# Griffin/PEER step on one core: the sample rows' experts divided over two blocks, four row places, one place for the slot tile

## The chip, the cores and the metric

The kernel runs on one NeuronCore of a Trainium2 chip. The metric is the device time of one execution in microseconds (us). Engines are named as in the profile: PE (matrix multiply, with PEld for its weight loads), DVE (vector), ACT (scalar/activation), POOL (here it issues the gathers by index), SP (it issues most DMAs). Each engine works through its own queue strictly in order, and engines wait for each other through semaphores.

## What is computed

One layer is applied to 1024 prompt rows and to 64 sample rows (8 sequences of 8) with the same weights:

```python
xn = rmsnorm(x)
xr, gr, q, k, v, ga, gb = split(xn @ w_in)
A = (rglru(conv(xr)) * gelu(gr)) @ w_branch_lru        # recurrent branch
B = window_attention(q, k, v) @ w_branch_attn          # sliding window, sinks
h = x + (sigmoid(ga) * A + sigmoid(gb) * B) @ w_out
# PEER on xt = rmsnorm(h): 8 heads x 16 experts out of 128*128 for each row
s = einsum('nhpd,hpkd->nhpk', (xt @ w_query), sub_keys)
idx, g = top16 of the sums of the two halves' top16, softmax
act = gelu(einsum('cd,ced->ce', xt, expert_u[idx])) * g
y = h + einsum('ce,ced->cd', act, expert_v[idx])
```

So each row needs 128 rows of `expert_u` and 128 rows of `expert_v`, chosen by its own scores.

## The kernel before

**Blocks.** The 1088 rows are cut into three blocks (`BLOCKS`), here called block 0 (256 prompt rows and the 64 sample rows), block 1 and block 2 (384 prompt rows each). `trunk(b)` works through one block: attention, the attention branch (its results `mg`, L322), the recurrent part `lru`, the recurrent branch (`th`, L337 and L338), `gh`/`gl` (L345, L346), `w_out` (its sums `hr`, L356), the second norm, and `retrieve` (the query projection and the top-16 search of `s`, L766 to L773). All projections go through `mm3`: three matmuls for each product of operands split in two parts, with weights streamed in pieces of 512 KB (`wraw`, `wlo`). After the three blocks, `dense` runs the prompt rows of blocks 0 and 1 against all 16384 experts, while the rows of block 2 gather theirs.

**Work behind a block.** What block b left for PEER is done during block b+1's trunk as a generator, `behind(b)`. `bg(k)` at each place of the trunk draws k steps from it, k from the table `PG1` while block 1 runs and `PG2` while block 2 runs (places 0 to 7: `mg` chunks, `lru` rounds, second branch, `w_out`, norm, `retrieve`, attention's projections, attention's scores). A scheduler then orders each engine's queue. The steps are:

- `choose(b)`: the candidates of block b's rows are reduced to 16 experts for each head; a step is either a search (max and index) or a pair of an `eq` (L822) and its minimum `ev` (L824). The sample rows come first, and their indices and weights go to `est`.
- for the sample rows alone `early_u` and `early_v`: 64 gathers of 128 rows each from `expert_u`, each multiplied and summed on DVE into one column of `eh` (L963), then gelu on `eh` (L965), then 64 gathers from `expert_v`, accumulated on DVE (L981), two final sums, and the store to `y`. The 64 sample rows stand twice in the 128 partitions, each half with 64 of the 128 experts.
- `build_g(b)`: the expert weights of the block's prompt rows are laid out as a dense table `g_d` for `dense`. It goes by chunks of 32 rows (8 chunks for block 0, 12 for block 1) and in each by products of 4 rows: DVE makes `oi` (L939), `oj` (L940) and `wi` (L941), PE multiplies (L922, four matmuls), ACT copies the result into `sg` (L923), and SP stores `sg` after 8 products (L925). The slot tile `sT` of a chunk is loaded by SP (L929).

**Shared places.** `sg`, the sample rows' gather places `et`, and attention's `at` are one buffer (tag `at`, one place). So `at_free` holds the early steps back until attention is over, and `sg` can't be written before the last reader of `et` is done. In `et`, one quarter holds the rows or the sum, and three quarters hold gathered rows:

```python
xt = et[:, 0:D]
row = et[:, D * (1 + s % 3):D * (2 + s % 3)]
sT = sp.tile([P, 3, CH], F32, tag="sT", name="sT", bufs=2)
```

Of the kernel before, what the change touches and what calls it, by code (L numbers as in the profile page):

```python
# [19 lines left out]
P = 128  # L20
# [41 lines left out]
PG1 = (6, 5, 4, 5, 2, 2, 0, 0)  # L62
PG2 = (5, 5, 4, 3, 2, 2, 2, 1)
# [11 lines left out]
class Kern:  # L75
# [325 lines left out]
    def attention(self, bi, xh, xl, ah, al, raw, bg):  # L401
# [46 lines left out]
        def scores(t, j, qT):  # L448
# [6 lines left out]
            for par in range(2):  # L455

                pss = self.mm().rearrange("p (g s) -> p g s", s=256)
                pr = slice(par * HD, par * HD + HD)
                for g2 in range(2):
                    nc.tensor.matmul(pss[:, g2, 0:S], qT[pr, 2 * j + g2, :], kT[pr, j, c0 + b0:c0 + 2 * P], start=True, stop=True)  # L460
                for g2 in range(2):
                    g = 2 * g2 + par
                    nc.vector.scalar_tensor_tensor(sb[:, g, 0:S], self.distP[:, b0:], -SLOPES[4 * j + g],
                                                   pss[:, g2, 0:S], op0=ALU.mult, op1=ALU.add)
# [312 lines left out]
    def choose(self, bi):  # L777
# [6 lines left out]
        for t, (c0, r) in sorted(enumerate(tiles), key=lambda x: x[1][1]):  # L784
# [31 lines left out]
            bf = xp.tile([P, PH, TOPK], F32, tag="bf", name="bf", bufs=1)  # L816
# [48 lines left out]
    def slots_T(self, ft, r, n0):  # L865

        nc = self.nc
        pt = self.tr((P, 3, P))
        for x in range(3):
            nc.tensor.transpose(pt[:, x, 0:r], ft[0:r, x], self.ident[0:r, 0:r])  # L870
        sl = self.xp.tile([P, 3, P], F32, tag="sl", name="sl", bufs=1)
        nc.scalar.copy(sl[:, :, 0:r], pt[:, :, 0:r])
        nc.sync.dma_start(self.sT_d[:, :, n0:n0 + r], sl[:, :, 0:r])
# [39 lines left out]
    def build_g(self, bi):  # L913
# [13 lines left out]
        for ch in range(COL0[bi] // CH, (COL0[bi] + nP) // CH):  # L927
            sT = sp.tile([P, 3, CH], F32, tag="sT", name="sT", bufs=2)
# [3 lines left out]
            for t4 in range(CH // 4):  # L932
# [5 lines left out]
                oi = sp.tile([P, P, 4], BF16, tag="oi", name="oi", bufs=2)  # L938
# [13 lines left out]
    def early_u(self):  # L952
# [3 lines left out]
        xt = et[:, 0:D]  # L956
        for a in range(2):
            nc.sync.dma_start(et[a * NS:(a + 1) * NS, 0:D], self.xn2n_d[NA:, :])
        for s in range(NSLOT // 2):
            row = et[:, D * (1 + s % 3):D * (2 + s % 3)]  # L960
# [8 lines left out]
    def early_v(self):  # L969
# [3 lines left out]
        acc = et[:, 0:D]  # L973
        row = lambda s: et[:, D * (1 + s % 3):D * (2 + s % 3)]
# [16 lines left out]
    def behind(self, b):  # L991

        early, left = False if b else None, True
        ch = self.choose(b)
        while left or early is not False:
            if early is None and self.es is not None and self.at_free:
                early = itertools.chain(self.early_u(), self.early_v())
            if left:
                left = next(ch, None) is not None
            for _ in range(2):  # L1000
                if early and next(early, None) is None:
                    early = False
# [206 lines left out]
```

## Time and profile before

| | |
|---|---|
| median of 3 runs (each) | 3769.24 us (3769.24, 3769.95, 3755.25) |
| the profiled execution | 3754.26 us, span of its trace 3752.5 us |
| busy share of the span | PE 89%, DVE 77%, POOL 41%, ACT 34% |
| DMA | 1012 MB moved, mean 270 GB/s |
| trunk of the three blocks | from 0 to about 1816 us |
| `dense` | from about 1816 us to the end |

PE's share is an average over stages with different limits. PE counts as busy while matmuls are in its pipeline. The stages of blocks 1 and 2 are read below by windows whose edges are the starts on DVE of the block's first `mg` (L322) and first `gl` (L346), of the end of a block's search (1284 and 1816). "The middle" of a block is the window from its first `mg` to its first `gl` (attention branch, `lru`, second branch), "the tail" what follows it (`w_out`, norm, `retrieve`).

### The profile page before, as it was taken

To read this page: it belongs to the slowest core of one execution; us is meant where nothing else is said; L and a number is where in the kernel's file an instruction comes from. 1 tells how busy PE (TensorE), PEld (TensorE's weight loads), DVE (VectorE), ACT (ScalarE), POOL (GpSimd) and SP (SyncE) were. 2 spreads that over 40 slices of the span, in tenths; PEclk is the share of its full clock that TensorE was granted. 3 is DMA by queue.
4 is the path that set the end of the run, shared out by engine and by line. 5 is a ranking of instruction groups with operands and counts; after the bars stand their busy time and mean duration, and the time that the engine had idled before them with its cause. 6 is when DMAs were issued, how large, how long until landed. Compare 5 with 4: busy or idle time off the path is not lost.

```text
span 3752.5 us, 58800 instructions
## 1 busy us (share of the span) xinstructions
PE 3336.7 (89%) x21891; PEld 3211.5 (86%) x21891; DVE 2882.6 (77%) x6803; ACT 1268.9 (34%) x2331; POOL 1520.3 (41%) x1240
## 2 busy tenths in 40 slices
PE   6899999883058989999889999999999999999996
PEld 6798988883058869998779999999999999999996
DVE  5567797984577988867899787777777776777777
ACT  4555454641033455743222222222222222222221
POOL 0011100223400000000367677677767776777774
PEclk8899999987579999999889999999999999999998
DMA  7388856998747627788488989989989888999988
GB/s 230 99 268 282 284 169 194 326 310 309 234 147 266 199 86 245 247 288 280 160 276 300 310 314 317 314 306 320 320 306 312 308 307 305 318 326 313 306 307 284
DMA packets 551327, 1012.37 MB, mean 270 GB/s; under 512 B 39452, under 2 KB 357852, under 8 KB 547936
## 3 DMA queue, kind: packets, MB, share of 16 engines
q1 hardware_dynamic: 409920, 494.75, 40.9%
q0 software_dynamic: 141120, 513.86, 38.5%
q8 instruction: 172, 2.82, 0.3%
q14 instruction: 115, 0.94, 0.1%
HBM read 904.14 MB, written 105.99 MB: 269 GB/s over the span
## 4 chain that ended last, share of the span: by engine, by line
PE 28%; DMA 18%; DVE 13%; issue 8%; POOL 7%; ACT 2%; SPq 0%; POOLq 0%; DVEq 0%; ACTq 0%
DMA row<-in_expert_v,iA 6%; DMA row<-in_expert_u,iA 4%; PE tr L922 3%; DMA et<-in_expert_v,est 3%; PE ou L183 3%; PE ou L184 3%; PE ou L185 3%; PE mm L185 3%; PE mm L183 3%; PE mm L184 3%; PE sc L183 3%; PE sc L184 3%; PE sc L185 3%; POOL row L888 2%; DVE row L890 2%
## 5 line engine op out<-in xcount | busy, mean ns | idle before, releaser
L183 PE MATMUL ou<-ah,vh 128*128 128x384 f32 (+1 forms) x2048 | 634.0, 314 | 42.5 <-ACT ah L163 20.2
L183 PE MATMUL sc<-dx,uh 128*128 128x256 f32 (+1 forms) x2048 | 637.7, 311 | 19.7 <-DVE al L164 10.3
L185 PE MATMUL sc<-dx,ul 128*128 128x256 f32 (+1 forms) x2048 | 635.9, 311 | 1.0 <-POOL ul L164 1.0
L184 PE MATMUL sc<-dx,uh 128*128 128x256 f32 (+1 forms) x2048 | 636.5, 311 | 0.0
L184 PE MATMUL ou<-al,vh 128*128 128x384 f32 (+1 forms) x2048 | 630.5, 310 | 1.9 <-DVE al L164 1.9
L185 PE MATMUL ou<-ah,vl 128*128 128x384 f32 (+1 forms) x2048 | 629.4, 310 | 0.5 <-POOL vl L164 0.5
L164 POOL TENSOR_TENSOR ul<-un,uh 128x1024 fp32r<-128x1024 f32 x128 | 308.2, 2408 | 790.3 <-ACT uh L163 787.4
L902 DVE SCALAR_TENSOR_TENSOR acc<-row,hv,acc 128x1024 f32<-128x1024 f32 x384 | 493.1, 1284 | 127.5 <-DMA row<-in_expert_v,iA 124.3
L890 DVE SCALAR_TENSOR_TENSOR row<-row,xt 128x1024 f32<-128x1024 f32 x384 | 465.0, 1216 | 138.7 <-DMA row<-in_expert_u,iA 136.5
L900 POOL DMA_INDIRECT row<-in_expert_v,iA x384 | 361.6, 942 | 278.6 <-DVE acc L902 202.9
L888 POOL DMA_INDIRECT row<-in_expert_u,iA x384 | 365.8, 953 | 265.5 <-DVE row L890 186.4
L183 PEld LDWEIGHTS ou<-ah,vh 128*128 128x128 f32 x2048 | 385.6, 190 | 59.8 <-DVE dac L1077 27.1
L183 PEld LDWEIGHTS sc<-dx,uh 128*128 128x128 f32 x2048 | 392.5, 192 | 21.4 <-DVE al L164 11.7
L185 PEld LDWEIGHTS sc<-dx,ul 128*128 128x128 f32 x2048 | 391.9, 191 | 1.5 <-POOL ul L164 1.5
L184 PEld LDWEIGHTS sc<-dx,uh 128*128 128x128 f32 x2048 | 392.3, 192 | 0.0
L184 PEld LDWEIGHTS ou<-al,vh 128*128 128x128 f32 x2048 | 388.1, 190 | 3.6 <-DVE al L164 2.7
L185 PEld LDWEIGHTS ou<-ah,vl 128*128 128x128 f32 x2048 | 387.6, 190 | 0.7 <-POOL vl L164 0.7
L922 PE MATMUL tr<-oij 128*128 128x128 f32 x1280 | 169.3, 288 | 202.4 <-ACT sg L923 200.7
L1077 DVE TENSOR_TENSOR dac<-dac,ou 128x384 f32<-128x384 f32 (+1 forms) x672 | 313.8, 481 | 38.2 <-PE ou L185 37.2
L922 PEld LDWEIGHTS tr<-oij 128*128 128x128 f32 x1280 | 164.6, 204 | 206.9 <-ACT sg L923 202.2
L164 POOL TENSOR_TENSOR vl<-vn,vh 128x1024 fp32r<-128x1024 f32 x128 | 309.2, 2420 | 14.6 <-ACT vh L163 12.6
L163 ACT CAST uh<-un 128x1024 fp32r<-128x1024 f32 x128 | 134.4, 1050 | 459.7 <-PE sc L184 360.9
(295 smaller groups left out, 7357.0 us busy)
## 6 DMA issues: line engine op xcount, KB each, us to landing
wlo<-lo_d SPq DMA_DIRECT2D x168, 512.0 KB, 4.9
wraw<-in_w_in SPq DMA_DIRECT2D x132, 512.0 KB, 5.9
un<-in_expert_uT SPq DMA_DIRECT2D x128, 512.0 KB, 5.9
vn<-in_expert_v SPq DMA_DIRECT2D x128, 512.0 KB, 5.8
lo_d<-wlo POOLq DMA_DIRECT2D x84, 512.0 KB, 6.0
g_d<-sg SPq DMA_DIRECT2D x20, 2048.0 KB, 6.9
wraw<-in_peer_w_query SPq DMA_DIRECT2D x48, 512.0 KB, 6.2
gt<-g_d SPq DMA_DIRECT2D x32, 768.0 KB, 10.3
```

What stands on the lines that cost most here:

```text
L163: nc.scalar.copy(hi, src)
L164: return (lo_eng or nc.vector).tensor_tensor(lo, src, f32(hi), op=ALU.subtract)
L183: nc.tensor.matmul(ps, lh, rh, start=first and j == 0, stop=False)
L184: nc.tensor.matmul(ps, lh, rl, start=False, stop=False)
L185: nc.tensor.matmul(ps, ll, rh, start=False, stop=last and j == n - 1)
L888: nc.gpsimd.indirect_dma_start(out=row, out_offset=None, in_=i["expert_u"], in_offset=bass.IndirectOffsetOnAxis(ap=ia[:, s:s + 1], axis=0))
L890: nc.vector.scalar_tensor_tensor(row, row, 1.0, xt, op0=ALU.mult, op1=ALU.mult, accum_out=hv[:, s:s + 1])
L900: nc.gpsimd.indirect_dma_start(out=row, out_offset=None, in_=i["expert_v"], in_offset=bass.IndirectOffsetOnAxis(ap=ia[:, s:s + 1], axis=0))
L902: nc.vector.scalar_tensor_tensor(acc, row, hv[:, s:s + 1], acc, op0=ALU.mult, op1=ALU.add)
L922: nc.tensor.matmul(pt[:, x, :], oj[:, x], wi[:, x], start=True, stop=True)
L1077: nc.vector.tensor_tensor(ac[k // 4][:, k % 4, a:b], ac[k // 4][:, k % 4, a:b], ps[:, 0:b - a], op=ALU.add)
```

## The change

`early_u` stays behind block 0, and so runs in block 1's trunk; `early_v` now runs behind block 1, in block 2's trunk. One early step is drawn with each step in place of two. `et` now has four places for gathered rows, and the rows `xt` and the sum `acc` have a tile of their own (tag `ex`). The room for it is found by giving `sT` and `oi` one place in place of two, and by letting `bf` share with `fi` and `sl` share with `cd`. The two tables change. In attention's `scores`, the four matmuls go in the order of the heads and so alternate between the two halves of the partitions and between two PSUM banks, and the DVE operations follow all four. Line numbers after L460 are lower by 2 in the changed kernel (L923 is L921 there).

```diff
-PG1 = (6, 5, 4, 5, 2, 2, 0, 0)
-PG2 = (5, 5, 4, 3, 2, 2, 2, 1)
+PG1 = (5, 5, 4, 5, 2, 2, 0, 0)
+PG2 = (6, 6, 5, 1, 2, 4, 2, 2)
...
-            for par in range(2):
-                pss = self.mm().rearrange("p (g s) -> p g s", s=256)
-                pr = slice(par * HD, par * HD + HD)
-                for g2 in range(2):
-                    nc.tensor.matmul(pss[:, g2, 0:S], qT[pr, 2 * j + g2, :], kT[pr, j, c0 + b0:c0 + 2 * P], start=True, stop=True)
-                for g2 in range(2):
-                    g = 2 * g2 + par
-                    nc.vector.scalar_tensor_tensor(sb[:, g, 0:S], self.distP[:, b0:], -SLOPES[4 * j + g],
-                                                   pss[:, g2, 0:S], op0=ALU.mult, op1=ALU.add)
+            pss = [self.mm().rearrange("p (g s) -> p g s", s=256) for _ in range(2)]
+            for g in range(4):
+                pr = slice(g % 2 * HD, g % 2 * HD + HD)
+                nc.tensor.matmul(pss[g % 2][:, g // 2, 0:S], qT[pr, 2 * j + g // 2, :], kT[pr, j, c0 + b0:c0 + 2 * P], start=True, stop=True)
+            for g in range(4):
+                nc.vector.scalar_tensor_tensor(sb[:, g, 0:S], self.distP[:, b0:], -SLOPES[4 * j + g],
+                                               pss[g % 2][:, g // 2, 0:S], op0=ALU.mult, op1=ALU.add)
...
-            bf = xp.tile([P, PH, TOPK], F32, tag="bf", name="bf", bufs=1)
+            bf = xp.tile([P, PH, TOPK], F32, tag="fi", name="bf", bufs=1)
...
-        sl = self.xp.tile([P, 3, P], F32, tag="sl", name="sl", bufs=1)
+        sl = self.xp.tile([P, 3, P], F32, tag="cd", name="sl", bufs=1)
...
-            sT = sp.tile([P, 3, CH], F32, tag="sT", name="sT", bufs=2)
+            sT = sp.tile([P, 3, CH], F32, tag="sT", name="sT", bufs=1)
...
-                oi = sp.tile([P, P, 4], BF16, tag="oi", name="oi", bufs=2)
+                oi = sp.tile([P, P, 4], BF16, tag="oi", name="oi", bufs=1)
...
-        xt = et[:, 0:D]
+        xt = self.sp.tile([P, D], F32, tag="ex", name="xt", bufs=1)
...
-            row = et[:, D * (1 + s % 3):D * (2 + s % 3)]
+            row = et[:, D * (s % 4):D * (s % 4 + 1)]
...
-        acc = et[:, 0:D]
-        row = lambda s: et[:, D * (1 + s % 3):D * (2 + s % 3)]
+        acc = self.sp.tile([P, D], F32, tag="ex", name="eacc", bufs=1)
+        row = lambda s: et[:, D * (s % 4):D * (s % 4 + 1)]
...
-        early, left = False if b else None, True
+        early, left = None, True
...
-                early = itertools.chain(self.early_u(), self.early_v())
+                early = self.early_v() if b else self.early_u()
...
-            for _ in range(2):
-                if early and next(early, None) is None:
-                    early = False
+            if early and next(early, None) is None:
+                early = False
```

On ACT in block 1, at the step from `gh` to `sg`, the queue before was this (`whi` are casts of weight pieces, here all eight of `w_out`):

```order
L345 ACTIVATE gh<-mg 128x384 x6
L208 CAST whi<-wraw 128x1024 x8
L965 ACT_TABLE_LOAD
L965 ACTIVATE eh<-eh 128x64
L923 COPY sg<-tr 128x128x4 x11
L931 CAST s_9206<-sT 128x32
L923 COPY sg<-tr 128x128x4 x8
```

and after the change it is this:

```order
L345 ACTIVATE gh<-mg 128x384 x8
L208 CAST whi<-wraw 128x1024 x2
L963 ACT_TABLE_LOAD
L963 ACTIVATE eh<-eh 128x64
L921 COPY sg<-tr 128x128x4 x6
L929 CAST s_8753<-sT 128x32
L921 COPY sg<-tr 128x128x4 x2
L208 CAST whi<-wraw 128x1024
```

The gelu of `eh` and the first `sg` copies moved from behind all of `w_out`'s weight casts to a place between them, and on DVE the 64 rows of `expert_v` no longer stand between `eh` and the last reader of `et`.

On DVE in block 1, the end of the early rows stood like this before:

```order
L963 SCALAR_TENSOR_TENSOR et,eh<-et 128x1024 x7
L966 TENSOR_TENSOR eh<-eh,est 128x64
L979 TENSOR_SCALAR et<-et,eh 128x1024
L981 SCALAR_TENSOR_TENSOR et<-et,eh 128x1024 x63
L986 TENSOR_TENSOR et<-et 64x1024
L987 TENSOR_TENSOR et<-et 64x1024
L940 TENSOR_TENSOR oij<-iof,sT 128x512
```

and after the change the end of `expert_v`'s rows stands in block 2, ahead of the first `gl`:

```order
L979 SCALAR_TENSOR_TENSOR eacc<-et,eh,eacc 128x1024 x2
L337 SCALAR_TENSOR_TENSOR th<-th,mm 128x384
L979 SCALAR_TENSOR_TENSOR eacc<-et,eh,eacc 128x1024
L338 TENSOR_TENSOR mg<-mg,th 128x384
L337 SCALAR_TENSOR_TENSOR th<-th,mm 128x384
L338 TENSOR_TENSOR mg<-mg,th 128x384
L984 TENSOR_TENSOR eacc<-eacc,et 64x1024
L346 SCALAR_TENSOR_TENSOR gl<-mg,gh 128x384 x3
L985 TENSOR_TENSOR eacc<-eacc,et 64x1024
```

The whole run of 63 rows left block 1's `w_out`, and its rows now stand one to three at a time between the trunk's operations of block 2's middle.

On DVE in block 2 after the change, the step from one chunk of `build_g` to the next behind `w_out` reads like this (`s_14962` and `s_15188` are the casts of the two chunks' `sT`):

```order
L937 TENSOR_TENSOR oi<-iota_208,s_14962 128x512
L939 TENSOR_TENSOR oij<-oi,sT 128x512
L938 TENSOR_TENSOR oij<-iof,sT 128x512 x6
L937 TENSOR_TENSOR oi<-iota_208,s_15188 128x512
L939 TENSOR_TENSOR oij<-oi,sT 128x512
```

and on PE behind `w_out` in block 2 the queue is this:

```order
L183 MATMUL mm<-whi,gh 128x256
L184 MATMUL mm<-wlo,gh 128x256
L185 MATMUL mm<-whi,gl 128x256
L920 MATMUL tr<-oij 128x128 x148
L267 MATMUL tr<-ident,xn 128x128 x8
L920 MATMUL tr<-oij 128x128 x8
```

Before, no more than three products (12 of these matmuls) stood together in block 2; now 37 products (148 matmuls) stand together between `w_out` and the norm's transposes, and the first `oj` of a chunk follows directly on the last `wi` of the chunk before, with one place for `sT`.

Counted in the order of DVE's queue:

| window | early rows (of them final sums) before, after | `oj` | `oi` | `wi` | `eq`/`ev` pairs | searches |
|---|---|---|---|---|---|---|
| middle of block 1 | 46, 60 | 9, 8 | 11, 7 | 9, 6 | 24, 24 | 24, 24 |
| tail of block 1 | 84 (2), 4 | 55, 56 | 53, 57 | 55, 58 | 0, 0 | 1, 1 |
| attention of block 2 | 0, 0 | 0, 0 | 0, 0 | 0, 0 | 8, 15 | 12, 15 |
| middle of block 2 | 0, 65 (1) | 73, 7 | 69, 8 | 67, 7 | 16, 9 | 11, 8 |
| tail of block 2 | 0, 1 (1) | 23, 89 | 27, 88 | 29, 89 | 0, 0 | 0, 0 |

## Rows read from the trace of the kernel before

**Rows 1.** The page: span, and granted TensorE clock in 40 slices (tenths).
```profile
span 3752.5 us, 58800 instructions
...
PEclk8899999987579999999889999999999999999998
```

**Rows 2.** Windows by stage: busy time (and instructions) of each engine, clock, DMA share, GB/s.
```profile
607.00:846.50 239.50, 214.89 (x1131) 204.02 (x1129) 210.26 (x592) 112.84 (x164) 52.38 (x49) 0.94 0.95 312
846.50:1284.00 437.50, 232.30 (x1680) 228.56 (x1680) 300.49 (x857) 106.94 (x186) 78.48 (x79) 0.77 0.70 237
1284.00:1386.00 102.00, 87.00 (x421) 61.41 (x422) 87.75 (x299) 59.14 (x178) 0.00 (x0) 0.93 0.20 60
1386.00:1652.00 266.00, 261.08 (x1656) 254.84 (x1654) 216.74 (x491) 146.15 (x235) 0.00 (x0) 1.00 0.78 255
1652.00:1816.00 164.00, 147.85 (x1018) 145.45 (x1018) 128.27 (x529) 53.04 (x83) 0.00 (x0) 0.93 0.71 244
1816.00:3752.50 1936.50, 1847.56 (x12328) 1824.52 (x12328) 1524.98 (x2681) 476.44 (x790) 1344.24 (x1024) 0.98 0.89 305
```

**Rows 3.** Windows: the tail of block 1 in three pieces, columns as above.
```profile
846.50:886.00 39.50, 35.97 (x285) 35.11 (x286) 21.14 (x41) 10.38 (x16) 11.45 (x11) 0.96 1.03 377
886.00:1062.00 176.00, 0.60 (x6) 0.39 (x4) 93.46 (x82) 2.58 (x3) 67.04 (x69) 0.52 0.73 231
1062.00:1284.00 222.00, 195.73 (x1392) 193.06 (x1392) 185.89 (x734) 93.97 (x167) 0.00 (x0) 0.93 0.63 217
```

**Rows 4.** Waits from 850 to 1100 us: total us, times, longest.
```profile
PE tr L922 <- ACT sg L923: 186.9, 3, 176.9
ACT sg L923 <- DMA out_y<-et: 156.2, 1, 156.2
...
DVE et L981 <- DMA et<-in_expert_v,est: 61.1, 60, 2.1
```

**Rows 5.** Tile `et`: ns min/median/max, first and last start us.
```profile
L963 DVE SCALAR_TENSOR_TENSOR et<-et x64: 1199/1219/1227, 654.7 to 905.1; 128x1024 f32<-128x1024 f32 x64
...
L981 DVE SCALAR_TENSOR_TENSOR et<-et,eh x63: 1283/1284/1341, 913.3 to 1053.1; 128x1024 f32<-128x1024 f32 x63
```

**Rows 6.** Groups by shape on DVE, 517 to 1816 us: busy us, mean ns, idle before.
```profile
L940 DVE TENSOR_TENSOR oij<-iof,sT 128x512 f32<-128x512 f32 x160 | 107.7, 685 | 33.9 <-PE tr L922 33.4
L941 DVE TENSOR_TENSOR oij<-oi,sT 128x512 f32<-128x512 bf16 x160 | 107.6, 682 | 0.0
...
L939 DVE TENSOR_TENSOR oi<-iota,s 128x512 bf16<-128x512 bf16 x160 | 64.5, 416 | 0.3
L822 DVE TENSOR_TENSOR eq<-ce,bf 128x800 f32<-128x800 f32 x40 | 39.4, 984 | 0.2
L824 DVE TENSOR_REDUCE ev<-eq 128x16 f32<-128x800 f32 x40 | 39.1, 978 | 0.2
```

**Rows 7.** Loads of `sT` (tile and its issuing line): durations, and issue to landing.
```profile
L929 SPq DMA_DIRECT2D sT<-sT_d x20: 519/530/2266, 712.6 to 1678.4; - x20
...
DMA to landing us min/median/max: 2.2/5.3/6.1
```

**Rows 8.** Tile `sg`: its store's time from issue to landing.
```profile
DMA to landing us min/median/max: 6.3/6.9/7.4
```

**Rows 9.** Timeline, DVE in block 2: five `oj` in a row.
```profile
1649.10 3.09 DVE L940 TENSOR_TENSOR oij<-iof,sT 128x512 f32<-128x512 f32 x5
```

**Rows 10.** The chain in order of time: start us, us, product matmuls merged.
```profile
1063.53 7.40 PE tr L922 x40
...
1596.14 2.68 PE tr L922 x24
```

**Rows 11.** Window inside block 1's middle, columns as in rows 2.
```profile
800.00:850.00 50.00, 48.52 (x295) 47.90 (x294) 41.24 (x87) 18.36 (x28) 12.59 (x11) 1.00 1.07 369
```

**Rows 12.** Score matmuls, line L460: ns min/median/max; PE idle before them, until whom.
```profile
L460 PE MATMUL mm<-at,qT x256: 272/376/792, 92.2 to 1349.8; 64*128 64x256 f32 x112, 64*128 64x128 f32 x16
...
DVE sb L463: 13.1, 18
```

**Rows 13.** The page's list of DMA issues: KB each, median us to landing.
```profile
g_d<-sg SPq DMA_DIRECT2D x20, 2048.0 KB, 6.9
```

More of the change, by code (lines that the diff above doesn't have):

```diff
@@ L955, in early_u @@
         et = self.sp.tile([P, AT], F32, tag="at", name="et", bufs=1)
-        xt = et[:, 0:D]
+        xt = self.sp.tile([P, D], F32, tag="ex", name="xt", bufs=1)
         for a in range(2):
-            nc.sync.dma_start(et[a * NS:(a + 1) * NS, 0:D], self.xn2n_d[NA:, :])
+            nc.sync.dma_start(xt[a * NS:(a + 1) * NS, :], self.xn2n_d[NA:, :])
         for s in range(NSLOT // 2):
-            row = et[:, D * (1 + s % 3):D * (2 + s % 3)]
+            row = et[:, D * (s % 4):D * (s % 4 + 1)]
             nc.gpsimd.indirect_dma_start(out=row, out_offset=None, in_=self.i["expert_u"],
```

## The prediction, written before the changed kernel ran

> **What bounds the kernel now.** I read the page first: TensorE's granted clock, near full over most of the span, falls to 7, 5 and 7 tenths around slice 10, inside block 1 [rows 1]. Then the windows by stage [rows 2]. The middles of both blocks and `dense` keep PE busy for 90 to 98% of their time. Block 1's tail doesn't: 437.5 us with 232 us of PE, where block 2's tail takes 164. Cut in three, that tail shows 176 us with 0.6 us of PE, at a clock of 0.52, between two pieces in which PE works [rows 3]. The waits name the chain: PE waits for ACT's `sg`, and ACT for the store of `y` out of `et` [rows 4]. Since `sg` and `et` are one buffer, the first `sg` must wait for all 64 rows of `expert_v`, and PE's products stand in front of everything else in its queue. The `expert_v` rows themselves run from 913.3 to 1053.1 [rows 5], 2.2 us each, and DVE waits 61 us for their landing [rows 4]: with three places the gathers' latency is the pace. Block 2's tail is the contrast: PE 148 of 164 us, DVE 128.
>
> The sum is made against the profiled execution, 3754.3 us (span 3752.5). The median of the three runs, 3769, lies 15 above it; one of the three, 3755, is within 1 of it. About 0.5% (19 us) is what a measurement can tell from no change.
>
> **The change, part by part.** Counts are those of the front's table, durations are means of rows.
>
> *A, tail of block 1.* 80 fewer early operations: 63 at 1.284 us, 14 `expert_u` rows at 1.22 [rows 5], the first of the `expert_v` rows and two final sums, at most 1.3 us each by the same rows, say 3 in all: -101 us of DVE. Products move by +1 `oj`, +4 `oi`, +3 `wi` at 0.685, 0.416 and 0.682 [rows 6]: +4. So DVE's 300.5 [rows 2] becomes 203. In the piece after the stall DVE was busy for 186 of 222 us, 84% [rows 3]; at that share 203 us take 242. `sT` with one place adds a wait between chunks (under E); here other DVE work stands at most of the seven steps, and the store of `sg` already waits at such steps, so I add 4. 246 us: **-192**. Bounds: 238 (share 0.85, no new wait) to 263 (all of 7 x 5.3, less what stands between: 18, and more idling): -200 to -175.
>
> *B, middle of block 1.* 14 more rows at 1.22 less 3 `wi`, 4 `oi`, 1 `oj`: +13 us on DVE, which is already busy for 210 of 239.5 us [rows 2]; with the column sums I take **+14** (+8 to +16).
>
> *C, attention of block 2.* PG2 draws 34 steps there in place of 22: 7 more pairs at 1.96 us [rows 6] and 3 more searches at under 1 us: +16 us of DVE in a stage where it is busy for 88 of 102 [rows 2]. **+16** (+10 to +18).
>
> The scores' new order moves no work. PE waited 13.1 us in all for banks that DVE had still to read [rows 12]; taking two of the three at once may double that, and gains can't pass the 14 us in which DVE idles there. Taken as 0, bounds -14 to +13.
>
> *D, middle of block 2.* PE loses 60 products of four matmuls at 2.68/24 = 0.112 us [rows 10]: -27 from 266 us. DVE gains 83 us of rows and loses 66 `oj`, 61 `oi`, 60 `wi` (112) and 16 of `choose`: about 172, so it no longer matters. DMA does: 255 GB/s x 266 us = 68 MB [rows 2], less 7.5 stores of `sg` at 2.1 MB [rows 13], plus 64 gathers of 0.52 MB: 86 MB. At 369 GB/s, the most that a busy stretch of block 1's middle shows [rows 11], that is 232 us; at that middle's mean of 312 [rows 2], 275. PE's 239 is between; I take 248, nearer the former as 312 is no ceiling: **-18** (-27 to +9). The gathers have nothing ahead of them on POOL; 64 rows in 248 us are 3.9 us each, against 2.2 with three places.
>
> *E, tail of block 2.* 66 `oj`, 61 `oi` and 60 `wi` come in; a run of five `oj` goes at 3.09/5 = 0.62 each [rows 9], a tenth under the mean, so 112 becomes 100, and DVE's 128 becomes 229 (one final sum more). DVE now leads PE (148). What is new is `sT`: SP can load a chunk's slots only once DVE has read the last of the chunk before, and DVE's next operation is the first that needs them. A load lands 5.3 us after its issue (2.2 to 6.1) [rows 7]. Eleven such steps have 4.5 us of other DVE work between them: 58 - 4.5 = 53 us of DVE waiting. The store of `sg` at the same steps (6.9 us [rows 8]) runs beside it and ends about when the next product is ready. Behind the waiting `oj` stand, on DVE, `w_out`'s sums, the norm and the search, and on PE, behind the products, the norm's transposes and `retrieve`'s matmuls; SP has behind the load the store of `sg` and the weights of `retrieve`. 229 + 53 + 4 for other waits = 286 against 164: **+122**. Lower bound: the load is covered after all and DVE is 95% busy, 241, +77. Upper: the new waits come on top of the 36 us that DVE idled there anyway, 318, +154.
>
> *F, start of `dense`.* The last eight products now stand behind the last search, and the first read of `g_d` waits for their store, 6.9 us [rows 8]: **+6** (0 to +12). The rest of `dense` has the same work in nearly the same order: 0.
>
> Sum: -192 + 14 + 16 - 18 + 122 + 6 = -52, so 3754 - 52 = **3702 us**.
>
> **Two rules weighed.** PE at low clock: the 176 us of idling ran at 0.52 and the piece behind it at 0.93 [rows 3]; at the low level a product matmul takes 7.40/40 = 0.185 us, at full 0.112 [rows 10]. The Trainium skill (TensorE: Matmul & The Clock Gate, What's actually happening) has it that the array is throttled by default and only activity releases it. By that rule the 37-product run, in which DVE feeds PE slowly, could put PE at 1.2 GHz again in block 2. That this case's mixed piece kept 0.93 speaks for less.
>
> The score matmuls of two partition halves take 376 ns each [rows 12], in a stage that DVE leads. The skill's TensorEngine Tiling (Array Packing), Key Properties, says that tiles on different rows can run in parallel; its Gotcha 1 adds that this raises the pressure on PSUM. By the first the sum falls by at most the 14 us above; by the second it grows by at most 13.
>
> **The rivals.**
> - *The slot loads are hidden*: another engine, not the load, ends the steps between chunks, so E is +77 and D -27: 3754 - 192 + 14 + 16 - 27 + 77 + 6 = 3648. For it: the store of `sg` is longer than the load and was waited for before. Against: no DVE work stands between most chunks. 0.22.
> - *Block 2's middle is bound by DMA*: D is +9 in place of -18: 3729. For it: 86 MB, and block 1's middle at a DMA share of 0.95 [rows 2]. Against: 369 GB/s was reached. 0.08.
> - *`expert_u` still comes late in block 1*: its rows went at (905.1 - 654.7)/63 = 4.0 us [rows 5] and 60 must now be done by the first `gl`, where 46 were. If the pace stays, the last ends as before, near 906, and PE idles for some 25 us after `w_out`'s first matmuls: 3727. Against: POOL waited for DVE, not for landings, and one step draws one row. 0.05.
> - *PE's clock falls in block 2's run of products*: 89 products x 4 x (0.185 - 0.112) = 26 us, if DVE hides none: 3728. The skill's rule would do this; most of it lies under DVE. 0.04.
> - *Slower: the stall only moves to block 2.* If `expert_v` rows are still to come when ACT reaches the first `sg` behind block 2's `gl`, PE stands as it did in block 1, at 2.2 us a row. From 3702 it takes 39 rows of the 64 to pass 3788; with all 64 the time is 3844. For it: weights and gathers share a nearly full DMA. Against: every row stands ahead of `gl` on DVE, so that rows slow the middle first, and they have 3.9 us each. 0.06.
>
> **How the numbers follow.** The forecast's own case (3665 to 3745) has 0.55, the rivals the rest. The lower bounds of all terms together give about 3608, the upper 3801; both are mishaps in a row, and the hidden loads' 3648 with some spread holds the low end, the two cases near 3728 the high one. The range is 3632 to 3768. Against the median of 3769, faster by over 0.5% means below 3750: most of the forecast (0.49), hidden loads (0.22), and most of the three cases near 3728 (0.14): 0.85. Within 0.5%: 0.09. Slower, above 3788: 0.06.
>
> **What would show it.** A: no wait of PE for `sg` over 10 us in block 1, its tail 235 to 265 us, the clock above 0.9 there. D: block 2's middle 240 to 260 us, DMA above 300 GB/s. E: DVE waiting for loads of `sT` about ten times, 50 us in all, block 2's tail 270 to 300 us, and PE below 60% busy. C: attention of block 2 at 115 to 120. I am wrong if DVE doesn't wait for `sT`, if block 2's tail is under 245 us, or if PE stands still for more than 20 us before the first `sg` of either block.

## The result, and the profile after

The changed kernel takes 3719.36 us (median of 3 runs, 3715.49 to 3723.01) against 3769.24. The ratio on record is 0.9887, 95% interval [0.9864, 0.9909]; the two medians alone would give 0.9868. In the runs of the next section the kernel before has medians of 3760 to 3761 us, so that 0.9887 stands for some 42 us. The forecast was 3702. The profiled execution is one of the three: 3715.49 us, span 3713.7. So it stands 38.8 us under the profiled execution of before, where the sum of the terms said 52.

The page of the changed kernel, span and granted TensorE clock, answers to [rows 1]:

```profile
span 3713.7 us, 58788 instructions
...
PEclk8899999989998999797999999999999999999998
```

The 7, 5, 7 around slice 10 are gone. Weaker dips, both of 7, stand now in slices 16 and 18 (counted from 0), in block 2's tail. The windows by stage (columns as in [rows 2], edges at the same instructions) say where the time went:

```profile
604.90:858.00 253.10, 219.70 (x1138) 205.18 (x1136) 222.23 (x610) 113.87 (x167) 70.32 (x63) 0.94 0.97 325
858.00:1112.60 254.60, 232.57 (x1685) 228.70 (x1686) 208.04 (x789) 106.35 (x182) 1.01 (x1) 0.93 0.74 248
1112.60:1218.00 105.40, 93.88 (x434) 66.60 (x433) 103.50 (x330) 58.17 (x174) 4.45 (x4) 0.88 0.21 65
1218.00:1458.50 240.50, 208.57 (x1113) 196.78 (x1111) 179.23 (x325) 106.98 (x156) 72.69 (x60) 0.97 1.01 337
1458.50:1757.30 298.80, 231.23 (x1541) 218.93 (x1539) 229.95 (x718) 94.80 (x164) 0.00 (x0) 0.85 0.56 198
1757.30:3713.70 1956.40, 1848.14 (x12328) 1822.67 (x12328) 1523.42 (x2680) 476.13 (x790) 1343.43 (x1024) 0.98 0.88 302
```

Against [rows 2]: block 1's tail -182.9 us, its middle +13.6, block 2's attention +3.4, middle -25.5, tail +134.8, and `dense` +19.9. The start, up to 604.9, is 2.1 shorter.

The waits of PE in block 1's tail answer to the 186.9 us of [rows 4], and tile `et` to [rows 5]:

```profile
PE tr L920 <- DVE rs_tk L197: 6.4, 1, 6.4
PE tr L920 <- DVE oij L939: 4.9, 1, 4.9
PE tr L920 <- ACT sg L921: 4.5, 3, 3.2
```

```profile
L961 DVE SCALAR_TENSOR_TENSOR et<-et,xt x64: 1167/1216/1227, 651.8 to 867.4; 128x1024 f32<-128x1024 f32 x64
...
L979 DVE SCALAR_TENSOR_TENSOR eacc<-et,eh,eacc x63: 1262/1280/1286, 1220.7 to 1448.9; 128x1024 f32<-128x1024 f32 x63
```

PE's wait for `sg` fell to 4.5 us. All rows of `expert_v` run before block 2's `gl` at 1458.5, at (1448.9 - 1220.7)/62 = 3.7 us each.

Block 2's tail is where most of it was given back. DVE's waits there (total us, times, longest):

```profile
DVE oij L938 <- DMA sT<-sT_d: 27.1, 11, 7.7
DVE v L766 <- PE tr L764: 19.4, 5, 6.0
DVE hr L356 <- DMA hr<-in_x_prompt: 8.4, 3, 6.7
```

The chain of work in order of time (start us, us), all loads of `sT` on it; below it windows over five of these loads, and two longer windows of the same tail:

```profile
1467.73 8.67 DMA sT<-sT_d
...
1490.85 2.35 DMA sT<-sT_d
...
1507.93 6.57 DMA sT<-sT_d
...
1533.29 7.30 DMA sT<-sT_d
...
1554.64 2.15 DMA sT<-sT_d
...
1570.98 2.26 DMA sT<-sT_d
...
1587.42 2.27 DMA sT<-sT_d
...
1604.95 3.34 DMA sT<-sT_d
```

```profile
1467.73:1476.40 8.67, 7.64 (x67) 7.43 (x66) 1.26 (x3) 2.22 (x3) 0.00 (x0) 1.00 1.07 415
1490.85:1493.20 2.35, 2.35 (x23) 2.35 (x22) 0.42 (x1) 0.58 (x1) 0.00 (x0) 1.00 0.16 28
1507.93:1514.50 6.57, 6.16 (x54) 5.95 (x53) 2.04 (x11) 4.52 (x8) 0.00 (x0) 1.00 1.04 359
1533.29:1540.59 7.30, 1.46 (x8) 1.17 (x8) 0.00 (x0) 0.58 (x1) 0.00 (x0) 0.52 1.04 322
1604.95:1608.29 3.34, 1.45 (x13) 1.21 (x11) 1.29 (x2) 1.80 (x4) 0.00 (x0) 1.00 0.56 123
```

```profile
1520.00:1540.00 20.00, 10.87 (x64) 9.59 (x64) 13.00 (x42) 4.68 (x8) 0.00 (x0) 0.76 0.79 252
1540.00:1560.00 20.00, 10.33 (x64) 9.87 (x64) 16.59 (x30) 5.12 (x10) 0.00 (x0) 0.67 0.38 159
```

DVE waited for the reload eleven times, as forecast, and eight of the loads are on the path. But the same 48 KB take 6.6 to 8.7 us where the DMA share over the load is 1.04 to 1.07, 3.3 us where it is 0.56, and 2.15 to 2.35 us where little else moves (0.14 to 0.16, four loads). Two of the three slow loads cost DVE only 1.1 and 1.0 us of waiting, since other work stood before the wait; the third cost 7.7.

### The profile page after: what moved, and what is told of

Its sections match the earlier page's. It is cut to its first block, busy times and chain, and to the rows that moved or that the text cites. A ratio compares the mean times of both kernels' runs of the same rounds, so it can differ in the third digit from the quotient of the medians.

```text
span 3713.7 us, 58788 instructions
## 1 busy us (share of the span) xinstructions
PE 3377.2 (91%) x21891; PEld 3226.7 (87%) x21891; DVE 2878.2 (78%) x6803; ACT 1271.7 (34%) x2330; POOL 1537.0 (41%) x1240
## 4 chain that ended last, share of the span: by engine, by line
PE 21%; DMA 16%; DVE 12%; issue 8%; POOL 7%; ACT 2%; SPq 0%; POOLq 0%; DVEq 0%; ACTq 0%
DMA row<-in_expert_v,iA 7%; DMA row<-in_expert_u,iA 3%; PE ou L183 3%; DVE row L888 3%; PE ou L184 3%; PE ou L185 3%; POOL row L886 3%; PE sc L183 2%; PE sc L185 2%; PE sc L184 2%; DVE acc L900 2%; POOL row L898 2%; PE mm L183 1%; PE mm L185 1%; PE mm L184 1%
## 5 line engine op out<-in xcount | busy, mean ns | idle before, releaser
L184 PE MATMUL ou<-al,vh 128*128 128x256 f32 (+1 forms) x2048 | 630.3, 310 | 1.9 <-DVE al L164 1.6
L185 PE MATMUL ou<-ah,vl 128*128 128x256 f32 (+1 forms) x2048 | 629.1, 310 | 0.0
L1074 DVE TENSOR_TENSOR dac<-dac,ou 128x384 f32<-128x384 f32 (+1 forms) x672 | 313.6, 480 | 43.5 <-PE ou L185 39.2
L164 POOL TENSOR_TENSOR vl<-vn,vh 128x1024 fp32r<-128x1024 f32 x128 | 309.2, 2420 | 14.6 <-ACT vh L163 11.8
L208 ACT CAST whi<-wraw 128x1024 fp32r<-128x1024 f32 x168 | 176.0, 1049 | 349.8 <-PE mm L184 201.4
L974 POOL DMA_INDIRECT et<-in_expert_v,est x64 | 77.1, 1205 | 495.6 <-PE pso L496 351.0
```

Of the source, the lines that this page charges most:

```text
L164: return (lo_eng or nc.vector).tensor_tensor(lo, src, f32(hi), op=ALU.subtract)
L184: nc.tensor.matmul(ps, lh, rl, start=False, stop=False)
L185: nc.tensor.matmul(ps, ll, rh, start=False, stop=last and j == n - 1)
L208: nc.scalar.copy(hi, raw)
L974: nc.gpsimd.indirect_dma_start(out=row(s), out_offset=None, in_=self.i["expert_v"], in_offset=bass.IndirectOffsetOnAxis(ap=self.es[:, 0, s ...
L1074: nc.vector.tensor_tensor(ac[k // 4][:, k % 4, a:b], ac[k // 4][:, k % 4, a:b], ps[:, 0:b - a], op=ALU.add)
```

## The experiments

Ratios are to runs of the kernel before on the same chip, beside those of the experiment. The changed kernel's is 0.9887. "Theory 1" and "rival" are those that each expectation names.

| run | median us | ratio [95%] |
|---|---|---|
| e1: changed, two `sT` places | 3669.13 | 0.9759 [0.9743, 0.9775] |
| e2: changed, three row places | 3745.15 | 0.9952 [0.9934, 0.9971] |
| e3: changed, old score order | 3717.05 | 0.9888 [0.9872, 0.9905] |
| e4: before + division + new tables | 3731.44 | 0.9932 [0.9913, 0.9952] |
| e5: before, one `sT` place | 3756.38 | 0.9988 [0.9970, 1.0007] |
| e6: changed, old tables | 3667.36 | 0.9742 [0.9721, 0.9763] |
| e7: changed, products in the search | 3713.04 | 0.9861 [0.9838, 0.9884] |
| e8: e1 and e7 together | 3687.30 | 0.9803 [0.9783, 0.9824] |
| e9: e6 and e1 together | 3672.45 | 0.9779 [0.9752, 0.9807] |
| e10: e9, two rows a step in block 2 | 3691.26 | 0.9821 [0.9800, 0.9842] |
| e11: before + division, own tables | 3727.30 | 0.9907 [0.9891, 0.9924] |
| e12: e9, no product left for `dense` | 3652.36 | 0.9709 [0.9684, 0.9733] |

**e1, two slot places.**

```diff
-            sT = sp.tile([P, 3, CH], F32, tag="sT", name="sT", bufs=1)
+            sT = sp.tile([P, 3, CH], F32, tag="sT", name="sT", bufs=2)
...
-                    s2 = self.sp.tile([P, P], F32, tag="s2", name="s2", bufs=1)
+                    s2 = self.sp.tile([P, P], F32, tag="ex", name="s2", bufs=1)
```

> The changed kernel with two places for the slot tile again; room for it comes from letting the search's scratch tile share with the tile of the sample rows. Eleven products move from behind the norm to beside w_out in block 2. Theory 1 (the reload of the one place costs DVE the 27 us of waits for it that the changed kernel's trace shows in block 2's tail, and DVE sets that tail): the waits go under 5 us, the tail falls from 299 to about 270 us, the whole from 3719 to about 3690. Rival (another wait ends the steps between chunks, the store of the finished chunk or PE at its low clock): the waits go, the tail stays above 290 us, the whole stays within 10 us of 3719.

Windows of block 1's tail and block 2's tail, and DVE's waits in the latter:

```profile
854.30:1097.50 243.20, 227.37 (x1686) 222.49 (x1686) 206.56 (x795) 106.20 (x181) 0.94 (x1) 0.96 0.76 259
...
1448.70:1720.50 271.80, 229.21 (x1538) 219.15 (x1538) 228.91 (x718) 91.78 (x162) 0.00 (x0) 0.87 0.61 217
```

```profile
DVE v L766 <- PE tr L764: 23.0, 5, 6.7
DVE oij L938 <- PE tr L920: 14.1, 21, 2.3
```

Theory 1 holds for the tail. DVE's work is the same (229 us), and the 27 us of waits and the tail's length went together. Block 1's tail lost another 11.4. In both tails one place was on the path. The whole fell by 50 us in the median, where 29 were expected; in the profiled executions the two tails are 38.4 of 44.8 us, and the rest is spread over other stages. Eleven products also changed their place within the tail, which by e7 and e8 below makes no difference. What DVE still waits for in this tail is PE (23.0 and 14.1 us).

**e2, three row places.** The same edit in `early_u` and `early_v`:

```diff
-            row = et[:, D * (s % 4):D * (s % 4 + 1)]
+            row = et[:, D * (s % 3):D * (s % 3 + 1)]
```

> The changed kernel with three places for gathered rows in place of four, all else as it is. In the queues 15 rows of expert_u (4 with four places) and 11 of expert_v (none) then stand behind the first gl. Theory 1 (places decide how many rows are through by gl, and PE's products stand in front of its queue until the rest are): PE waits for sg some 20 us in each block's tail, 11 rows at 2 us, and the whole is 3719 + 35 = 3755, nearly the kernel before. Rival (a row takes 3.6 to 3.9 us in the middles with four places, above the 2.2 us that three gave, so places don't matter): 3719, within 10 us.

Waits behind `gl` in block 1 (first row) and in block 2 (second), and the windows of the two tails:

```profile
PE tr L920 <- ACT sg L921: 21.6, 3, 14.8
```

```profile
PE tr L920 <- ACT sg L921: 13.9, 2, 12.6
```

```profile
845.30:1126.80 281.50, 235.04 (x1694) 229.03 (x1693) 220.35 (x813) 108.88 (x188) 12.27 (x12) 0.93 0.71 245
...
1453.50:1793.00 339.50, 242.42 (x1544) 227.53 (x1544) 245.68 (x730) 95.31 (x166) 9.50 (x8) 0.84 0.54 191
```

The fourth place matters. By the counts of the queues it lets the order put the rows ahead of `gl`, and PE's waits of 21.6 and 13.9 us were 4.5 and 0.7 with four places. It also lands rows in better time: DVE's waits for rows, over both blocks, are 27.0 us with three places and 11.9 with four. With three, the tails are 26.9 and 40.7 us longer and the middles 14.1 and 18.6 shorter. That makes 34.9 us net between the profiled executions, theory 1's 35, but e2's is the second slowest of its seven; by the ratios it is 0.9952 - 0.9887 = 0.0065, some 24 us. Either is more than the rival's 10.

**e3, old score order.** The block of `scores` is that of before:

```diff
-            pss = [self.mm().rearrange("p (g s) -> p g s", s=256) for _ in range(2)]
-            for g in range(4):
...
+            for par in range(2):
+                pss = self.mm().rearrange("p (g s) -> p g s", s=256)
...
```

> The changed kernel with the order of the score matmuls from before. In the changed kernel the attention of block 2 took 105 us with 103.5 us of DVE, though DVE had 16 us more work there than before, which took 102. Theory 1 (the new order closes DVE's gaps): with the old order that stage is 113 us or more, block 1's attention 91 or more, and the whole 5 to 20 us longer. Rival (the added steps fill the gaps by themselves, whatever the order): 105 us within 3, 91 within 2, and the whole within 5 us of 3719.

Block 2's attention:

```profile
1114.20:1221.80 107.60, 91.55 (x414) 63.72 (x414) 103.33 (x321) 58.20 (x173) 4.96 (x4) 0.88 0.19 59
```

The rival holds: 107.6 against 105.4 us, the whole at 0.9888. No effect of the order shows. PE waited 13.3 us in all for banks in the changed kernel, 10.5 here and 13.1 before [rows 12], and a score matmul has a median of 376 ns in all three.

e3 also shows how far a single window can be trusted. Its edit is in attention alone, yet block 2's middle is 247.9 us against 240.5 and its tail 289.9 against 298.8. A window is read from one execution, so a difference of up to some 9 us in one stage is not shown by it alone.

**e4 and e11, the division alone**, with the new tables and with its own:

```diff
-        early, left = False if b else None, True
+        early, left = None, True
...
-                early = itertools.chain(self.early_u(), self.early_v())
+                early = self.early_v() if b else self.early_u()
...
-            for _ in range(2):
-                if early and next(early, None) is None:
-                    early = False
+            if early and next(early, None) is None:
+                early = False
```

> The kernel before with the division of the early rows over the two blocks and the two new tables alone: three row places, two slot places, the old order of scores. Behind the first gl stand 18 rows of expert_u in block 1 and 9 of expert_v in block 2. Theory 1 (the stall of 177 us is what the change takes away, and the division does that alone, but the rows behind gl give part back): block 1's tail about 275 us, block 2's about 290 us, the whole 3725 to 3750. Rival (the division is all there is, and two slot places make it better than the changed kernel): 3700 or less. Second rival (without the fourth place nothing is gained): 3769 within 10 us.

> The kernel before with the division alone: its own tables, three row places, two slot places, the old order of scores. By its queues 18 rows of expert_u and 11 of expert_v stand behind the gl of their block, no product beside w_out in block 2, 47 behind the norm, 34 in the search, five in dense. Theory 1 (the new tables, not the one place, made most of block 2's long tail): 20 us or more under the 3731 of the same kernel with the new tables. Rival (with three places the rows behind gl set the tail, and tables matter little): within 10 us of 3731.

e4 falls into theory 1's span (3731). Its tails are 289.1 and 324.0 us: without the fourth place 18 and 9 rows stand behind `gl`. e11 differs from it by 4 us in the median, not 20, and the rival's size holds, but not its reason: e11's search ends at 1755.2 us and e4's at 1779.7, so the old tables gained 24 us in the trunk. The five products left for `dense` took it back: its first multiplication by the table comes 41 us behind the search (e4: 17). e12 below takes that up.

**e5, one slot place in the kernel before.**

```diff
-            sT = sp.tile([P, 3, CH], F32, tag="sT", name="sT", bufs=2)
+            sT = sp.tile([P, 3, CH], F32, tag="sT", name="sT", bufs=1)
```

> The kernel before with one place for the slot tile and nothing else changed: the price of that part by itself. Theory 1 (one place costs where DVE leads and its next operation needs the new chunk): block 2's middle and tail, where PE leads, stay within 5 us, block 1's tail takes 5 to 15 us more (the changed kernel gave back 11 there with two places), the whole 5 to 20 us more than the kernel before. Rival (the place always costs its reload, 53 us over the steps from chunk to chunk, wherever they stand): 30 us more or worse.

DVE's waits in block 2 of that kernel:

```profile
DVE oij L940 <- DMA sT<-sT_d: 20.0, 6, 7.1
```

There are waits of 20.0 us in block 2 and 6.9 in block 1's tail, yet the time is that of before (0.9988), which rules out the rival. Theory 1 is right on block 2 (middle 265.7 us against 266.0, tail 167.5 against 164.0), where PE leads and DVE's wait is free, and wrong on block 1's tail, for which it had 5 to 15 us more: it took 433.5 against 437.5. So the place had no measurable price of its own: it got one in the changed kernel, where DVE's waits lengthen both tails (e1).

**e6, the old tables in the changed kernel.**

```diff
-PG1 = (5, 5, 4, 5, 2, 2, 0, 0)
-PG2 = (6, 6, 5, 1, 2, 4, 2, 2)
+PG1 = (6, 5, 4, 5, 2, 2, 0, 0)
+PG2 = (5, 5, 4, 3, 2, 2, 2, 1)
```

> The changed kernel with both tables of before. By its queues all 64 rows of expert_v still stand ahead of the second gl; of the 89 products behind it 35 (in place of 25) stand in block 2's search, 43 (in place of 64) beside w_out and the norm, 14 in the middle, and the last four at the start of dense; block 2's attention has 8 eq/ev pairs in place of 15. Theory 1 (products beside w_out and the norm are paid for in full by DVE, those in the search are hidden by PE's 80 us of full work there): block 2's tail 270 to 285 us in place of 299, attention 97 in place of 105, the whole about 3700. Rival (the new tables are what keeps the rows ahead of gl and the whole short): 3730 or more.

Attention, middle and tail of block 2, and DVE's wait for `sT` in that tail:

```profile
1103.50:1210.90 107.40, 91.47 (x422) 64.80 (x421) 88.22 (x301) 60.24 (x176) 3.74 (x4) 0.89 0.23 70
1210.90:1462.50 251.60, 219.03 (x1197) 204.60 (x1196) 204.58 (x386) 114.47 (x169) 80.39 (x60) 0.97 1.01 337
1462.50:1719.90 257.40, 212.57 (x1417) 205.52 (x1417) 212.27 (x687) 83.77 (x144) 0.00 (x0) 0.88 0.58 203
```

```profile
DVE oij L938 <- DMA sT<-sT_d: 12.5, 8, 5.3
```

This was a surprise in size: 52 us in the median, 40 between the profiled executions. The new tables cost about as much as the one slot place (0.9742 here, 0.9759 in e1). With the old ones DVE has 25 us more work in block 2's middle, where it had 61 us to spare, and the middle grows by 11. The tail is 41 us shorter. DVE has 18 us less work in it, as 11 products are no longer there (seven are in the middle and four at the start of `dense`). The rest is idle time of DVE: its waits for `sT` fall by 14.6 us and those for the search's scores from 19.4 to 5.2. Why these fall too isn't separated from the work that moved, nor is `PG1` from `PG2`. The attention, with 15 us less of DVE, took 2 us more: at 88 us of DVE's work that stage isn't set by it.

**e7 and e8, products moved into the search**, with one slot place and with two:

```diff
-PG2 = (6, 6, 5, 1, 2, 4, 2, 2)
+PG2 = (6, 6, 3, 0, 0, 6, 2, 2)
```

> The changed kernel with PG2 = (6, 6, 3, 0, 0, 6, 2, 2) alone: 26 of the products that stood behind w_out and the norm now stand in block 2's search, with one slot place. Theory 1 (the search keeps PE full for 80 us while DVE has some 28 us free there, so a product costs DVE nothing extra in it, and 1.8 us outside): 26 x 1.8 = 47 us less in front, some 20 more in the search: block 2's tail 299 - 27 = 272 us, the whole about 3692. Rival (the search is as full for DVE, since it waits for sT there as well): the tail within 8 us of 299.

> Both: two slot places and PG2 = (6, 6, 3, 0, 0, 6, 2, 2). Theory 1 (the two gains add, since one takes DVE's waits and the other its work out of the stretch behind w_out): tail of block 2 about 240 us, the whole 3669 - 27 = 3642. Rival (once DVE no longer waits, PE's own work ends the tail: 229 us busy, and it is full in the search): the tail at 260 us or more, the whole 3655 or more.

The rivals hold in both. e7's tail took 300.1 us, e8's 272.2, the same as with the products behind the norm (298.9 and 271.7). The median of e8 is no better than e1's (3687 against 3669). In e7 PE is still full from 1580 to 1660 us while DVE is busy for 53 of these 80 us: DVE's queue is in order and waits for the search's scores (20.3 us in the tail), so products behind them run later, when DVE is full anyway; that is my reading, and no run tests it by itself. In e8 DVE waits for PE instead (19.9 us for the products, 19.2 for the scores), as its rival had it. Moving 26 products within the tail changed nothing that can be measured. What helped was to take products out of the tail, as e6 did.

**e9 and e10: both gains, and rows drawn faster.** e9 has the edits of e1 and e6; e10 adds to it:

```diff
-            if early and next(early, None) is None:
-                early = False
+            for _ in range(1 + b):
+                if early and next(early, None) is None:
+                    early = False
```

> The changed kernel with both tables of before and with two slot places. In its queues 19 products stand in block 2's middle, 77 waiting places go down to 73 in its tail (22, 16 and 35 beside w_out, norm and search), four in dense. Theory 1 (the tables' cost and the one place's cost are different waits of DVE, so they add, but the old tables alone left only 12.5 us of waits for sT in block 2's tail): 12 us there and 10 in block 1's tail less than the 3667 of the old tables: about 3645. Rival (both took the same idle time of DVE away): 3660 to 3670.

> As the run with old tables and two slot places, but two early rows are drawn with each step while block 2 runs. In the queues all 64 rows of expert_v then stand in the first part of block 2's middle, and 71 products behind them in the same middle, as many as in the kernel before; 25 are left for the tail. Theory 1 (DVE is what pays for products in the tail, and the middle has the room): the middle is then set by DVE, 64 x 1.28 + 71 x 1.8 + 100 of its own = 310 us in place of 250, the tail falls to about 170 us, and the whole is some 30 us under the run with one row a step: about 3615. Rival (rows and weights share a full DMA, so rows that are asked for sooner land late and hold DVE's queue and so PE): the middle 340 us or more, the whole 3650 or more.

The search ends at 1757.3 us in the changed kernel, at 1720.5 in e1, 1719.9 in e6 and 1691.8 in e9. So in the trunk the two gains nearly add (36.8 and 37.4 us alone, 65.5 together), as theory 1 had it. The whole did not follow: 3672 against e6's 3667, in the rival's size, where theory 1 had 3645. In e9's profiled execution the rest of `dense` took 21 us more than in e6's, of which more below. e10 is the rival's case in its size. Its middle and a piece of it, with PE's waits:

```profile
1194.70:1563.00 368.30, 270.17 (x1644) 259.73 (x1642) 296.36 (x550) 147.50 (x237) 71.47 (x60) 0.87 0.83 277
```

```profile
1320.00:1360.00 40.00, 2.07 (x8) 1.78 (x8) 32.12 (x31) 0.48 (x1) 23.03 (x21) 0.51 0.84 282
```

```profile
PE tr L920 <- ACT sg L921: 53.0, 1, 53.0
PE tr L868 <- DVE ft L854: 28.7, 1, 28.7
```

The tail is 169.6 us as theory 1 had it, but the middle is 368 and not 310. The products drawn early stand in PE's queue before the last rows are through, so the stall of the kernel before is back, in block 2's middle. Late rows, the rival's reason, show little: DVE waits 15.4 us for them in this middle, and is busy for 32 of the 40 us in which PE stands.

**e12, nothing left for `dense`.** e9 with one number more in the search:

```diff
-PG2 = (5, 5, 4, 3, 2, 2, 2, 1)
+PG2 = (5, 5, 4, 3, 2, 3, 2, 1)
```

> As the run with old tables and two slot places, with PG2 = (5, 5, 4, 3, 2, 3, 2, 1): three steps for each round of the search in place of two, so that the four products that stood at the start of dense stand in the search; all else in the queues of block 2 as there. In the three runs with four or five products in dense, its first multiplication by the table came 39 to 41 us behind the last search; in the others 14 to 18. Theory 1 (those products, their store and the table's load behind it cost dense 22 us): the first one at 17 us, the search 5 to 8 us longer, the whole 15 us under that run: about 3655. Rival (the products cost as much DVE time in the search, and dense starts late for another reason): the whole within 5 us of 3672.

The middle and the tail of block 2:

```profile
1195.80:1450.80 255.00, 224.32 (x1230) 209.51 (x1228) 213.26 (x403) 116.57 (x173) 80.77 (x60) 0.97 1.01 339
1450.80:1695.10 244.30, 207.60 (x1450) 202.12 (x1449) 207.20 (x684) 86.02 (x149) 0.00 (x0) 0.93 0.63 225
```

The multiplications by the table in `dense` (first and last start), of e9 and then of e12, and DVE's wait at the start of e9's `dense`:

```profile
L1052 DVE TENSOR_TENSOR sc<-sc,gt x256: 406/487/567, 1730.7 to 3610.8; 128x256 f32<-128x256 f32 x128
```

```profile
L1052 DVE TENSOR_TENSOR sc<-sc,gt x256: 406/484/567, 1713.2 to 3594.7; 128x256 f32<-128x256 f32 x128
```

```profile
DVE fi L784 <- DMA g_d<-sg: 14.2, 1, 14.2
```

Theory 1 holds for the start of `dense`: with four products behind the last search, the first multiplication comes 1730.7 - 1691.8 = 38.9 us behind it, with none 1713.2 - 1695.1 = 18.1, and the tail grew by 5.7 (expected: 5 to 8). At 0.9709 [0.9684, 0.9733] this run has the lowest ratio of all, 67 us under the changed kernel by the medians. Its interval is clear of those of e1 and e9, but touches that of e6 ([0.9721, 0.9763]).

## Why the prediction was right, and where its steps were off

The sum was 13.2 us too low. Against their terms the parts came to +9.1 (A), -0.4 (B), -12.6 (C), -7.5 (D), +12.8 (E), +13.9 (`dense`) and -2.1 (the start): misses of 36 us one way and 23 the other. The mechanism held, but that the sum came so near is in part luck.

**What bounded it, and A.** The main step held. The stall came from the rows of `expert_v` behind `gl`, and it is gone. The tail took 254.6 us against 246 (-183 for -192). The 8.6 us are the term for one slot place, put at 4: e1's two places give 243.2, the 242 of 203/0.84 (11.4 us), and DVE waits in this tail 4.7 us for `sT` and 9.0 for its cast. e2 adds what the working missed: rows had to be ahead of `gl` in the queue, and the fourth place put them there. With three, 15 and 11 stay behind it. The division does the main work: in e4, with three places, block 1's tail is down from 437.5 to 289.1 us.

**B** was +13.6 for +14.

**C was wrong in kind, at little cost:** +3.4 for +16. DVE got its 16 us (87.75 to 103.50), but the stage didn't grow by them: they filled idle time of DVE, of which 14 us stood there before and 2 after. In e6, with 88.2 us of DVE, it took 107.4. I had taken DVE's 86% share for the bound of that stage; it was not. What bounds it stays open. The scores' order was rightly put at 0 (e3). The trace shows neither a gain from tiles on other rows nor more waiting for banks, so it sides with neither of the two rules weighed there from the Trainium skill (TensorEngine Tiling (Array Packing), Key Properties and Gotcha 1).

**D**: -25.5 for -18, with DMA the bound as said: a share of 1.01 at 337 GB/s. PE's busy time fell by 52.5 us, where 27 were forecast; the reason stands under E.

**E was mis-sized inside, nearly right in sum:** +134.8 for +122. DVE's work was 230 us (229 forecast). The eleven waits for `sT` came to 27.1, not 53. The 5.3 us of [rows 7] is the middle of only three loads, those whose landing the trace tells: two beside full traffic (6.1 and 5.3) and one in a quiet stretch (2.2). Here most loads fell into quiet stretches, and two of the slow ones had other DVE work before the wait. The "4 for other waits" were 299 - 230 - 27 = 42, above all the search's scores (19.4) and the loads of `hr` (8.4). The 36 us that DVE idled in this tail before, which stood only in the upper bound, should have been in the sum. The two errors, -26 and +38, nearly cancel, which is luck.

PE was busy for 77%, not under 60%. Here the prediction misread a row: it took [rows 10] for one piece to each of a product's four matmuls. The trace before has 1280 PE pieces for the 160 products of [rows 6], eight to a product:

```profile
L922 PE MATMUL tr<-oij 128*128 128x128 f32 x1280 | 169.3, 288 | 202.4 <-ACT sg L923 200.7
```

So a product takes 8 x 0.112 = 0.9 us of PE, twice what D, E and the rival on PE's clock reckon with. In this tail the products' PE time rose from 31.0 to 107.2 us. D and E changed little by it, since they were sized by DMA and DVE. But over this tail PE (231 us) is as busy as DVE (230), so that DVE "now leads PE" is too simple: once `sT` has two places, DVE waits for PE (e1).

**F and the rest of `dense`**: +20 for +6. The start of `dense` isn't it: the first multiplication by the table comes 16 us behind the edge before and 16.9 after. The products that I counted behind the last search were done before it: the last copy into `sg` starts at 1723.1, the search ends at 1757.3. The 19 us lie spread over the rest, from that multiplication to the end: 1920.5 us before, 1939.5 after. Seven kernels with the same `dense` (before, after, e1, e6, e9, e11, e12) gave 1920.5, 1939.5, 1930.9, 1915.0, 1935.6, 1933.0 and 1937.3. It follows none of the changes that were tried. PE's waits in it for ACT's `ah` and for DVE's sums `dac` (L1077, now L1074) grew from 36.2 us before to 56.3 after, as much as the 19 us; what drove them, no run shows. The kernel before alone spread from 3745.52 to 3772.87 us over 13 runs, so this may be no more than the difference of two executions.

**The rivals.** That the slot loads are hidden fell (e1). That block 2's middle grows under DMA fell: it shrank. That `expert_u` comes late fell: its rows went at (867.4 - 651.8)/63 = 3.4 us, the last one 9 us behind the first `gl`, and PE's longest wait for `sg` was 3.2 us. PE's clock did fall in the run of products, to 0.67. The Trainium skill (TensorE: Matmul & The Clock Gate, What's actually happening) has it that the array is throttled by default and that activity releases it, and this trace agrees. Most of the fall was covered, as PE stood 35.9 us waiting for DVE in this tail. Not all of it: at 1594.69 the chain has 32 pieces of products in 5.62 us, 0.176 each, near the low level's 0.185. The stall that moves to block 2 didn't come, but was near: e2 has 11 rows of it, e10 a wait of 53 us.

**What the forecast didn't ask:** whether the tables were good. It priced the steps that they moved (C, E) one by one, and never set a product's 1.8 us of DVE in the tail, where DVE's work and waits set the length, against the same 1.8 us in block 2's middle, where DVE had 61 us to spare. The old tables are worth 0.9887 - 0.9742 = 0.0145 of the time (e6), more than the 0.0113 that the whole change gained. Of their 41 us in the tail, 18 are such work; the rest are waits that went with it.

## What to carry to other kernels

When a shared buffer makes a matmul queue wait, count which instructions stand ahead of the release in each queue: one more place can pay by moving work across that line, and not only by hiding latency. Take a load's latency from a row with the traffic of the place where it will run, count how many loads that row rests on, and keep the idle time that a stage already had in its new sum. Before a count is multiplied by a duration, check that the trace's pieces and the program's instructions are the same things. A busy share near 90% doesn't show that an engine sets a stage: add or remove work there, or find whose wait ends last.

## What the runs showed of the hardware that was not expected

- A 48 KB load took 2.15 to 2.35 us from its issue where little else moved (DMA share over the load 0.14 to 0.16), 3.34 us at 0.56, and 6.6 to 8.7 us at 1.04 to 1.07 (the changed kernel).
- While 64 gathers of 0.52 MB ran beside the streamed weights, DMA held 328 to 339 GB/s over 240 to 255 us at a share of 0.99 to 1.01, in five kernels (the changed kernel, e1, e3, e6, e12).
- With PE busy for 2 of 40 us the clock was 0.51, about the low level of 1.2 GHz (e10); in stretches of 20 us with PE busy for 10.3 and 10.9 us, between products that DVE feeds, its mean was 0.67 and 0.76 (the changed kernel).
- The four float32 matmuls of a product stand in the trace as eight pieces on PE (1280 for 160 products, the kernel before).
